# A two-layer hybrid decoder block on one core: both token tiles take turns on each tile of feed-forward weights, w2 in one-unit blocks, and a new order table

## The chip, the cores and the metric

The kernel runs on one core of a Trainium2 chip. The metric is the device time of one execution, in microseconds (us). Five engines matter: TensorE (PE, with its weight loads as PEld), VectorE (DVE), ScalarE (ACT), GpSimd (POOL) and SyncE (SP), which here issues the DMAs. The kernel before has a median of 1520.91 us.

## The reference

Two layers of a post-norm decoder, for 256 tokens of width 1024, all in float32 (a is a constant):

```
x = LN1(a*x + 0.5 * (silu(x @ w1) * (x @ w3)) @ w2)     FFN1, w1 and w3 1024 x 2816, w2 2816 x 1024
x = LN2(a*x + W_o(sum_i sigmoid(g_i(x)) * y_i(x)))      four gated token mixers: gMLP, short conv, MLA, NSA
x = LN3(a*x + CrossAttn(x, mem))                        4 heads over 256 memory rows
x = LN4(a*x + 0.5 * SwiGLU_2(x))                        FFN2, shapes of FFN1
```

## The kernel before

**Tiles.** The 256 tokens are two tiles of 128 (tile 0 and tile 1; `x_65` and `x_66` in the listings). A float32 product is made of three matmuls, from a high part and a low part of each operand: high by high (L256), high by low (L257), low by high (L258). For a feed-forward product the transposed tokens (`xh`, `xl`) are the operand that is loaded into TensorE and 512 columns of weights run past it.

**Weights.** They stream from memory once, in pieces of 128 x 1024 float32 (512 KB, two k-tiles of 512 columns each, or one k-tile of 1024 columns). A piece goes through three steps: a DMA issued by SP brings `raw` (4 buffers), ACT casts it to the high part `wh` (L244), DVE subtracts to get the low part `wl` (L245). `wh` and `wl` have 8 buffers each, the ring: a piece can be cast only when the piece that stood 8 before it has had its last matmul, and a `raw` buffer is free when its `wl` is made.

**A feed-forward.** Its 2816 hidden columns are five groups of 512 and one of 256 (`gi` 0 to 5 in `ffn`). In a group tile 0 first goes through all the pieces of w1 and w3 and then tile 1 does; only the first group of the whole kernel is written with both tiles at once. After a tile's two sums ACT makes `sil` (L407) and DVE `h` (L409), and `h` is transposed on TensorE a little later (it is deferred, and let out by `flush` within a later `group`). Then `wide` multiplies by w2: pieces ("units") of 2 k-tiles in blocks of 2, 3, 3 and 3 units, in each block tile 0 first, then tile 1, each with two 512-column sums. The layer norm (L361 to L369) adds the sums to x, and `to_xT` transposes x for the next stage.

**PSUM.** Three `acc` banks, one `oacc`, two `tr` (transposes) and two `att`.

**Order.** The program is not issued in the order of the code. `issue_order` takes a list per engine from the table `ISSUE`: numbers of the engine's instructions in program order, in the order in which they are to run. An engine runs its list strictly in order, so an instruction that waits holds up all that stand behind it on that engine. SP's list orders the DMA issues.

Other names below: `za`, `zb`, `zc`, `zd` are the first products of the mixing part, taken out of PSUM by DVE with a bias (L801, to `zza`, `zzb`, `zzc`, `zzd`); `gg`, `gb`, `bs`, `ws` are gMLP's parameters; `mq` is the rotated query (L466), `T` the gated sum of the mixers (L870), `xoh` the high part of the cross-attention output (L291), `xpT` its transposed probabilities (L972).

Of the kernel before, what the change touches and what calls it, by code (L numbers as in the profile page):

```python
# [17 lines left out]
P = 128  # L18
# [4 lines left out]
FF = 2816  # L23
# [4 lines left out]
NT = SEQ // P  # L28
KD = D // P
# [133 lines left out]
class Build:  # L163
# [38 lines left out]
    def acc(self):  # L202
        return self.ps.tile([P, 512], F32, name=self.nm("acc"), tag="acc", bufs=3)
# [172 lines left out]
    def ffn(self, l, which, lnw, last=False):  # L376
# [3 lines left out]
        for gi in range(6):  # L380
# [7 lines left out]
            first = len(self.plan) <= 4 and {t: (self.acc(), self.acc() if t == 0 else self.oacc()) for t in range(NT)}  # L388
            if first:
                for j, us in enumerate((u1, u3)):  # L390
                    for i, (get, k) in enumerate((get, k) for nk, get in us for k in range(nk)):
                        for t in range(NT):
                            self.mm3(first[t][j], *self.xT[t](i), *get(k, 0, w), i == 0, i == KD - 1)
            for t in range(NT):
                self.stream = "af"[t]
                if first:
                    pa, pb = first[t]
                elif w == 512:
                    pa, pb = self.acc(), self.acc() if t == 0 else self.oacc()
                    self.group(pa, self.xT[t], u1, 0, w)  # L400
                    self.group(pb, self.xT[t], u3, 0, w)
                elif w < 512:
                    both = self.acc()
                    self.group(both, self.xT[t], u13, 0, 2 * w)
                    pa, pb = both[:, :w], both[:, w:]
                sil = self.s("sil", w)
                nc.scalar.activation(sil, pa, AF.Silu)  # L407
                h = self.s("h", w)
                nc.vector.scalar_tensor_tensor(h, pb, 0.5, sil, op0=ALU.mult, op1=ALU.mult)  # L409
                hT[t, gi] = hh, hl = self.s("hh", w, F32R), self.s("hl", w, F32R)  # L410
                self.stream = "a"

                def back(h=h, hh=hh, hl=hl, w=w):
                    ps = self.transposes([h[:, i * P:(i + 1) * P] for i in range(w // P)])
                    self.split(ps[:, :w], hh, hl)
                self.later.append(back)
# [4 lines left out]
        out = self.wide(w2, l, FF // P, src, (2, 3, 3, 3))  # L421
# [604 lines left out]
def issue_order(tc, nc):  # L1026
# [3 lines left out]
    for engine in ENGINES:  # L1030
# [275 lines left out]
```

## Time and profile before

| what | value |
|---|---|
| median of 3 runs | 1520.91 us (1519.75 to 1523.56) |
| profiled execution, own time | 1518.77 us |
| its span, first to last instruction | 1517.0 us |
| mean granted TensorE clock | 0.998 |
| busy share PE, PEld, DVE, ACT | 98%, 82%, 66%, 47% |
| DMA queue of the weights, share of 16 engines | 55.2% |

The profile is one execution. Its own time is 2.1 us below the median, and 1.8 us above its span. A busy share counts the time from an instruction's start to its modelled end, and matmuls overlap, so the share says where TensorE is never idle and not how fast it goes; where it waits, a row of the trace carries the idle time and what ended it in square brackets.

### The profile page before, as it was taken

What the parts mean: (1) busy time and instruction counts of PE and PEld (TensorE: products, weight loads), DVE (VectorE), ACT (ScalarE), POOL (GpSimd) and SP (SyncE); (2) the same over time, 40 slices, a digit from 0 to 9 for tenths busy, and PEclk for the clock granted to TensorE, in tenths of its full rate; (3) what the DMA queues carried; (4) which work ended last, traced back from release to release, by engine and by line L of the source; (5) the groups of instructions that cost most, each with busy time, mean ns of one, the idle gap of its engine ahead of it and who ended that gap; (6) DMA issues with size and microseconds to landing.
All of it is one profiled execution on the core that took longest, in us unless ns stands there. A gap on an engine that the chain in (4) does not pass through costs nothing.

```text
span 1517.0 us, 20797 instructions
## 1 busy us (share of the span) xinstructions
PE 1488.4 (98%) x7994; PEld 1243.5 (82%) x7994; DVE 999.5 (66%) x1390; ACT 715.6 (47%) x1061; POOL 52.8 (3%) x48
## 2 busy tenths in 40 slices
PE   8999999999999999999999999999999999999998
PEld 6888788987887888878878887889778879888786
DVE  5555577888687776644665545787777777864535
ACT  5444433555456354543445443445555554554431
POOL 0000000000010000000000000000001100000000
PEclk9999999999999999999999999999999999999999
DMA  7566656445365554646556576654444565466533
GB/s 251 191 211 235 227 166 225 151 160 177 114 219 182 175 172 156 206 159 227 168 176 202 164 244 207 203 196 162 155 152 149 194 195 194 137 204 202 190 130 111
DMA packets 83187, 278.29 MB, mean 183 GB/s; under 512 B 10256, under 2 KB 11920, under 8 KB 83088
## 3 DMA queue, kind: packets, MB, share of 16 engines
q1 hardware_dynamic: 83088, 276.96, 55.2%
q8 instruction: 63, 1.03, 0.3%
q14 instruction: 36, 0.29, 0.1%
HBM read 275.88 MB, written 1.05 MB: 183 GB/s over the span
## 4 chain that ended last, share of the span: by engine, by line
PE 85%; DMA 7%; DVE 4%; ACT 2%; issue 1%; SPq 0%; POOL 0%; DVEq 0%; ACTq 0%
PE acc L256 21%; PE acc L258 21%; PE acc L257 21%; DMA raw<-in_wflat_dram 6%; PE oacc L257 4%; PE oacc L256 4%; PE oacc L258 4%; PE tr L306 4%; DVE wl L245 3%; ACT wh L244 2%; PE att L508 2%; PE oacc L521 1%; PE att L256 1%; PE att L258 1%; PE att L257 1%
## 5 line engine op out<-in xcount | busy, mean ns | idle before, releaser
L245 DVE TENSOR_TENSOR wl<-raw,wh 128x1024 fp32r<-128x1024 f32 (+4 forms) x487 | 585.6, 1220 | 289.8 <-ACT wh L244 280.9
L244 ACT CAST wh<-raw 128x1024 fp32r<-128x1024 f32 (+4 forms) x487 | 499.7, 1040 | 410.9 <-PE acc L258 247.8
L256 PE MATMUL acc<-wh,xh 128*128 128x512 f32 (+2 forms) x1008 | 389.8, 393 | 6.7 <-ACT wh L244 4.3
L257 PE MATMUL acc<-wl,xh 128*128 128x512 f32 (+2 forms) x1008 | 389.5, 390 | 0.6 <-DVE wl L245 0.6
L258 PE MATMUL acc<-wh,xl 128*128 128x512 f32 (+2 forms) x1008 | 388.3, 389 | 0.0
L256 PEld LDWEIGHTS acc<-wh,xh 128*128 128x128 f32 x1008 | 188.5, 188 | 48.5 <-ACT wh L244 8.5
L257 PEld LDWEIGHTS acc<-wl,xh 128*128 128x128 f32 x1008 | 189.8, 188 | 38.0 <-DVE wl L245 2.5
L258 PEld LDWEIGHTS acc<-wh,xl 128*128 128x128 f32 x1008 | 189.8, 188 | 36.4 <-issue 0.3
L257 PE MATMUL acc<-wl,hh 128*128 128x512 f32 x264 | 101.6, 392 | 1.7 <-DVE wl L245 1.7
L258 PE MATMUL acc<-wh,hl 128*128 128x512 f32 x264 | 101.9, 390 | 0.0
L256 PE MATMUL acc<-wh,hh 128*128 128x512 f32 x264 | 100.7, 396 | 0.0
L256 PE MATMUL acc<-xh,wh 128*128 128x256 f32 x320 | 90.8, 287 | 2.0 <-DVE zv L801 1.8
L257 PE MATMUL acc<-xl,wh 128*128 128x256 f32 x320 | 90.4, 285 | 0.0
L258 PE MATMUL acc<-xh,wl 128*128 128x256 f32 x320 | 90.0, 284 | 0.0
L256 PE MATMUL oacc<-wh,xh 128*128 128x512 f32 x176 | 69.7, 396 | 0.6 <-ACT wh L244 0.6
L257 PE MATMUL oacc<-wl,xh 128*128 128x512 f32 x176 | 69.4, 394 | 0.2 <-DVE wl L245 0.2
L258 PE MATMUL oacc<-wh,xl 128*128 128x512 f32 x176 | 69.3, 393 | 0.0
L256 PEld LDWEIGHTS acc<-xh,wh 128*128 128x128 f32 x320 | 61.0, 192 | 3.1 <-issue 2.5
L329 POOL TENSOR_TENSOR rstd<-var,cst 128x1 f32<-128x1 f32 x28 | 23.9, 860 | 1091.4 <-DVE var L328 1090.7
L257 PEld LDWEIGHTS acc<-xl,wh 128*128 128x128 f32 x320 | 61.2, 191 | 0.6 <-issue 0.3
L258 PEld LDWEIGHTS acc<-xh,wl 128*128 128x128 f32 x320 | 61.2, 192 | 0.1
L256 PEld LDWEIGHTS acc<-wh,hh 128*128 128x128 f32 x264 | 49.0, 188 | 13.9 <-ACT wh L244 4.9
(247 smaller groups left out, 1899.7 us busy)
## 6 DMA issues: line engine op xcount, KB each, us to landing
raw<-in_wflat_dram SPq DMA_DIRECT2D x465, 512.0 KB, 5.0
bias<-in_rows_dram SPq DMA_DIRECT2D x22, 256.0 KB, 5.6
lng<-in_rows_dram SPq DMA_DIRECT2D x8, 512.0 KB, 6.2
lnb<-in_rows_dram SPq DMA_DIRECT2D x8, 512.0 KB, 6.3
raw<-in_wflat_dram SPq DMA_DIRECT2D x8, 416.0 KB, 3.8
wc<-in_small_dram SPq DMA_DIRECT2D x8, 256.0 KB, 6.1
memr<-in_memt_dram SPq DMA_DIRECT2D x8, 256.0 KB, 6.0
raw<-in_wflat_dram SPq DMA_DIRECT2D x4, 420.0 KB, 3.4
```

Of the source, the lines that this page charges most:

```text
L244: nc.scalar.copy(hi[:, :m], raw[:, :m])
L245: nc.vector.tensor_sub(lo[:, :m], raw[:, :m], hi[:, :m])
L256: mm(out, ah, bh, start=start, stop=False, skip_group_check=True)
L257: mm(out, ah, bl, start=False, stop=False, skip_group_check=True)
L258: mm(out, al, bh, start=False, stop=stop, skip_group_check=True)
L306: self.nc.tensor.transpose(t[:rows, i * part:(i + 1) * part], s, self.ident[:part, :part])
L329: nc.gpsimd.tensor_tensor(y, v, self.c("mhalf"), op=ALU.pow)
L508: nc.tensor.matmul(ps[:, i * nk + s * P:i * nk + (s + 1) * P], qT(h0 + i), kT(h0 + i, s), start=True, stop=True, skip_group_check=True)
L521: nc.tensor.matmul(place(h), vT(h, s), p, start=s == 0 and start(h), stop=last and s == t, skip_group_check=True)
```

## The change

Three edits. First, in `ffn` the two tiles take turns on each k-tile of w1 and w3 (`turns`), in every group but the first one of the three later feed-forwards; the four sums are then open together, and deferred transposes are let out twice within a pass. Second, w2 runs in one-unit blocks, eight of them and a last one of three units: after each unit of 2 k-tiles the other tile follows on the same two pieces. Third, the table `ISSUE` is new for every engine, in all parts of the program. The arithmetic is the same: the same products, additions and DMAs.

```diff
-            first = len(self.plan) <= 4 and {t: (self.acc(), self.acc() if t == 0 else self.oacc()) for t in range(NT)}
-            if first:
-                for j, us in enumerate((u1, u3)):
-                    for i, (get, k) in enumerate((get, k) for nk, get in us for k in range(nk)):
-                        for t in range(NT):
-                            self.mm3(first[t][j], *self.xT[t](i), *get(k, 0, w), i == 0, i == KD - 1)
+
+            turns = gi > 0 or len(self.plan) <= 4
+            acc = lambda j, t: self.oacc() if j and t else self.acc()
+            ps = {}
+            if w == 512:
+                parts = [(j, us) for j, us in enumerate((u1, u3))]
+            else:
+                parts = [(0, u13)]
+            wide = 512
+            if turns:
+                for j, us in parts:
+                    for t in range(NT):
+                        ps[t, j] = acc(j, t)
+                    i = 0
+                    for nk, get in us:
+                        for k in range(nk):
+                            for t in range(NT):
+                                self.mm3(ps[t, j], *self.xT[t](i), *get(k, 0, wide), i == 0, i == KD - 1)
+                            i += 1
+                            if i in (DEFER, DEFER + 2):
+                                self.flush()
             for t in range(NT):
                 self.stream = "af"[t]
-                if first:
-                    pa, pb = first[t]
-                elif w == 512:
-                    pa, pb = self.acc(), self.acc() if t == 0 else self.oacc()
-                    self.group(pa, self.xT[t], u1, 0, w)
-                    self.group(pb, self.xT[t], u3, 0, w)
...
+                if not turns:
+                    for j, us in parts:
+                        ps[t, j] = acc(j, t)
+                        self.group(ps[t, j], self.xT[t], us, 0, wide)
...
-        out = self.wide(w2, l, FF // P, src, (2, 3, 3, 3))
+        out = self.wide(w2, l, FF // P, src, (1,) * 8 + (3,))
...
 ISSUE = {
     "PE":
-        "0-10 13 11-12 16 14 17-18 15 22 19-21 25 23-24 28-30 34-35 26-27 31-33 36 40-42 46 37 47-48 52-54 38-39 "
...
     "Pool":
-        "0-1 6-7 2-5 8-11 13 15 14 12 16-23 28-29 24-27 30-43",
+        "0-1 6-7 2-5 8-11 13-15 12 16-23 28-29 24-27 30-31 33-34 32 35-43",
```

Three places of the orders follow; the numbers behind a name tell copies apart. The first is TensorE in FFN1 of layer 0, second group of columns (`gi` = 1). `wh_280` and `wh_286` are pieces of w1, `wh_292` and `wh_304` pieces of w3; `acc_314` is tile 0's sum with w1. Before:

```order
L256 MATMUL acc_314<-wh_280,xh 128x512
L257 MATMUL acc_314<-wl_281,xh 128x512
L258 MATMUL acc_314<-wh_280,xl 128x512
L256 MATMUL acc_314<-wh_280,xh 128x512
L257 MATMUL acc_314<-wl_281,xh 128x512
L258 MATMUL acc_314<-wh_280,xl 128x512
L256 MATMUL acc_314<-wh_286,xh 128x512
```

After, where `acc_378` is tile 0's sum with w3 and `oacc_379` tile 1's:

```order
L256 MATMUL acc_378<-wh_304,xh 128x512
L256 MATMUL oacc_379<-wh_292,xh 128x512
L257 MATMUL acc_378<-wl_305,xh 128x512
L257 MATMUL oacc_379<-wl_293,xh 128x512
L258 MATMUL acc_378<-wh_304,xl 128x512
L258 MATMUL oacc_379<-wh_292,xl 128x512
L256 MATMUL acc_378<-wh_304,xh 128x512
L256 MATMUL oacc_379<-wh_292,xh 128x512
```

Before, one tile runs through a new piece every 6 matmuls; after, both tiles are on pieces that stand two apart, and a new piece is needed every 12.

The second place is DVE at the start of layer 0's mixing part: `wl_2086` to `wl_2098` are weights of `turned` products that run later, `zzc` are the additions that empty the PSUM banks of `zc`. Before:

```order
L245 TENSOR_TENSOR wl_2086<-raw_2083,wh_2085 128x1024
L245 TENSOR_TENSOR wl_2092<-raw_2089,wh_2091 128x1024
L801 TENSOR_TENSOR zzc_1772<-acc_1747,bias_1721 128x416
L801 TENSOR_TENSOR zzc_1799<-acc_1774,bias_1721 128x416
L245 TENSOR_TENSOR wl_2098<-raw_2095,wh_2097 128x1024
```

After:

```order
L245 TENSOR_TENSOR wl_2086<-raw_2083,wh_2085 128x1024
L814 TENSOR_TENSOR zzc_1772<-acc_1747,bias_1721 128x416
L814 TENSOR_TENSOR zzc_1799<-acc_1774,bias_1721 128x416
L245 TENSOR_TENSOR wl_2092<-raw_2089,wh_2091 128x1024
L245 TENSOR_TENSOR wl_2098<-raw_2095,wh_2097 128x1024
```

The two additions stand one weight piece earlier.

The third place is TensorE where FFN1 of layer 0 ends: `wh_1394` and `wh_1400` are the last pieces of w2, `x_65` is tile 0 after the layer norm, `acc_1586` the first sum of `za`. Before:

```order
L306 MATMUL tr_1491<-ident,x_65 128x128 x4
L257 MATMUL acc_1073<-wl_1395,hh_1065 128x512
L256 MATMUL acc_1074<-wh_1394,hh_1065 128x512
L258 MATMUL acc_1073<-wh_1394,hl_1066 128x512
L257 MATMUL acc_1074<-wl_1395,hh_1065 128x512
L256 MATMUL acc_1073<-wh_1400,hh_1065 128x512
L258 MATMUL acc_1074<-wh_1394,hl_1066 128x512
L257 MATMUL acc_1073<-wl_1401,hh_1065 128x512
L306 MATMUL tr_1498<-ident,x_65 128x128 x4
```

After:

```order
L256 MATMUL acc_1069<-wh_1394,hh_1060 128x512
L257 MATMUL acc_1069<-wl_1395,hh_1060 128x512
L258 MATMUL acc_1069<-wh_1394,hl_1061 128x512
L256 MATMUL acc_1069<-wh_1400,hh_1060 128x512
L257 MATMUL acc_1069<-wl_1401,hh_1060 128x512
L258 MATMUL acc_1069<-wh_1400,hl_1061 128x512
L306 MATMUL tr_1491<-ident,x_65 128x128 x4
L306 MATMUL tr_1498<-ident,x_65 128x128 x4
L256 MATMUL acc_1586<-wh_1538,xh 128x512
```

Tile 0's transposes moved from among the last w2 matmuls to behind them, and the product that reads them follows at once. Tile 1's transposes (`x_66`) stood 48 issues behind `wh_1538`'s first matmul and now stand 16 behind it.

Moves that are told in words: the DMAs of `gg`, `gb`, `bs` and `ws` stood between the last pieces of w2 on SP's list and now stand behind them, and in layer 1 DVE's `ws` operation (L721, now L734) stands behind the last `wl` of w2 instead of ahead of `wl_8049`; SP issues `raw_100` ahead of the tokens at the start; the cross-attention products of tile 1 and its transposes stand some 4 us of matmuls earlier; `mq`'s rotation is no longer split by other DVE work; in the last layer norm DVE's list had L368 twice and then L369 twice, and has L368, L369, L368, L369 after.

## Rows read from the trace of the kernel before

**Rows 1.** The page, busy time of each engine over the span.

```profile
PE 1488.4 (98%) x7994; PEld 1243.5 (82%) x7994; DVE 999.5 (66%) x1390; ACT 715.6 (47%) x1061; POOL 52.8 (3%) x48
```

**Rows 2.** TensorE's waits: us in total, times, longest us.

```profile
PE acc L256 <- ACT wh L244: 4.3, 5, 1.9
PE acc L257 <- DVE wl L245: 2.3, 3, 1.7
PE acc L256 <- DVE zzc L801: 2.1, 2, 1.5
PE tr L306 <- DVE mq L466: 1.4, 2, 0.9
PE acc L976 <- ACT xpT L972: 1.4, 2, 0.7
PE acc L256 <- ACT xoh L291: 1.4, 2, 0.7
PE oacc L256 <- ACT wh L244: 1.3, 3, 0.7
PE tr L306 <- DVE T L870: 0.8, 1, 0.8
PE oacc L257 <- DVE wl L245: 0.7, 2, 0.5
PE acc L258 <- DVE oCl L292: 0.5, 1, 0.5
PE acc L306 <- DVE h L409: 0.3, 1, 0.3
```

**Rows 3.** Timeline of PE in FFN1, steady: start us, us, instruction.

```profile
111.42 0.39 PE L256 MATMUL acc<-wh,xh 128*128 128x512 f32 x1
111.65 0.39 PE L257 MATMUL acc<-wl,xh 128*128 128x512 f32 x1
```

**Rows 4.** Timeline of PE at the supply waits of layer 0's FFN1.

```profile
23.24 0.39 PE L258 MATMUL acc<-wh,xl 128*128 128x512 f32 x1
24.48 0.73 PE L256 MATMUL acc<-wh,xh 128*128 128x512 f32 x2 [0.85 <-ACT wh L244]
...
30.78 0.73 PE L256 MATMUL acc<-wh,xh 128*128 128x512 f32 x2 [0.44 <-ACT wh L244]
32.04 0.50 PE L257 MATMUL acc<-wl,xh 128*128 128x512 f32 x1 [0.30 <-DVE wl L245]
```

**Rows 5.** Groups of DVE and ACT by form: count, busy us, mean ns, idle before.

```profile
L245 DVE TENSOR_TENSOR wl<-raw,wh 128x1024 fp32r<-128x1024 f32 x465 | 566.8, 1237 | 284.8 <-ACT wh L244 276.0 <-DMA raw<-in_wflat_dram 0.4
...
L244 ACT CAST wh<-raw 128x1024 fp32r<-128x1024 f32 x465 | 482.9, 1053 | 396.9 <-PE acc L258 237.4 <-DMA raw<-in_wflat_dram 68.7 <-PE oacc L258 35.1
...
L291 ACT CAST xh<-tr 128x512 fp32r<-128x512 f32 x28 | 15.8, 587 | 52.8 <-PE tr L306 52.6
```

**Rows 6.** The chain that ended last, at the end of layer 1's FFN1.

```profile
925.13 7.68 DMA ws<-in_small_dram
```

**Rows 7.** Timeline of DVE at layer 0's `zzc`.

```profile
233.93 1.23 DVE L245 TENSOR_TENSOR wl<-raw,wh 128x1024 fp32r<-128x1024 f32 x1 [1.96 <-ACT wh L244]
235.07 1.08 DVE L801 TENSOR_TENSOR zzc<-acc,bias 128x416 f32<-128x416 f32 x2
```

**Rows 8.** Timeline of ACT in layer 1's FFN2, w2.

```profile
1427.90 1.06 ACT L244 CAST wh<-raw 128x1024 fp32r<-128x1024 f32 x1 [0.30 <-PE acc L258]
1429.26 1.05 ACT L244 CAST wh<-raw 128x1024 fp32r<-128x1024 f32 x1 [0.30 <-PE acc L258]
```

**Rows 9.** Timeline at the end, behind the last matmul.

```profile
1509.49 0.69 DVE L361 SCALAR_TENSOR_TENSOR x<-x,acc 128x512 f32<-128x512 f32 x1 [2.22 <-PE acc L258]
...
1511.25 1.40 DVE L368 SCALAR_TENSOR_TENSOR x<-x,mv,lng 128x512 f32<-128x512 f32 x2
1511.48 0.92 POOL L329 TENSOR_TENSOR rstd<-var,cst 128x1 f32<-128x1 f32 x1 [7.78 <-DVE var L328]
1512.57 1.41 DVE L369 SCALAR_TENSOR_TENSOR x<-x,rstd,lnb 128x512 f32<-128x512 f32 x2
```

More of the change, by code (lines that the diff above doesn't have):

```diff
@@ L387, in ffn @@
                 u13 = self.cols((w1, w3), l, c0, 2 * w, KD)
-            first = len(self.plan) <= 4 and {t: (self.acc(), self.acc() if t == 0 else self.oacc()) for t in range(NT)}
-            if first:
-                for j, us in enumerate((u1, u3)):
-                    for i, (get, k) in enumerate((get, k) for nk, get in us for k in range(nk)):
-                        for t in range(NT):
-                            self.mm3(first[t][j], *self.xT[t](i), *get(k, 0, w), i == 0, i == KD - 1)
+            turns = gi > 0 or len(self.plan) <= 4
[18 more added lines that the diff above has]
+                                self.flush()
             for t in range(NT):
                 self.stream = "af"[t]
-                if first:
-                    pa, pb = first[t]
-                elif w == 512:
-                    pa, pb = self.acc(), self.acc() if t == 0 else self.oacc()
-                    self.group(pa, self.xT[t], u1, 0, w)
-                    self.group(pb, self.xT[t], u3, 0, w)
[L402 to L405, printed above, removed]
+                if not turns:
+                    for j, us in parts:
+                        ps[t, j] = acc(j, t)
+                        self.group(ps[t, j], self.xT[t], us, 0, wide)
+                if w == 512:
+                    pa, pb = ps[t, 0], ps[t, 1]
+                else:
+                    pa, pb = ps[t, 0][:, :w], ps[t, 0][:, w:]
                 sil = self.s("sil", w)
```

388 rows, old and new, of the table ISSUE are left out of this document.

## The prediction

> **What bounds the kernel now.** I read the page first: TensorE is busy 98% of the span, the others far less [rows 1]. Neither that share nor a faster engine elsewhere says what can be won; what can is TensorE's idle time, so the view that counts is its list of waits [rows 2]. The rows there that the change can reach add up to 16.5 us in 26 waits. The timeline of a steady stretch gives the pace: a 512-column matmul starts every 0.23 us [rows 3], and a piece of weights lasts 12 of them, 2.7 us, when both tiles use it together, but 1.36 us when one tile runs through it alone. The groups show what a piece costs to make: 1.05 us on ACT, 1.24 us on DVE, and that most of ACT's idle time ahead of its casts ends with a matmul, that is, with a slot of the ring coming free, not with a DMA [rows 5]. So the ring is the supply's limit in most places, and the order decides how often a piece is wanted right behind the one whose slot it takes.
>
> A wait costs more than its idle time: at the first one of FFN1 the starts are 1.24 us apart, 1.01 more than the pace, with 0.85 us idle [rows 4]. I add 0.16 us per wait throughout.
>
> **The change part by part.** The instructions are the same in number and shape on every engine that matters, so no busy time is added or removed; the sum is made of waits.
>
> *Feed-forwards in turns (FFN1).* Layer 0 has three waits at 24 to 32 us, 0.85, 0.44 and 0.30 us [rows 4], all in the second group, where tile 0 alone runs through eight new pieces at 1.36 us each. In the new order that group starts some 30 issues later, and counting 0.227 us per matmul, no slot in either FFN1 is wanted less than 4 us after its old piece's last use; before, 20 pieces of layer 0 and 23 of layer 1 were wanted within 2.6 us. A cast and a subtraction together take 2.3 us, so those waits go: 1.59 + 3 x 0.16 = 2.1 us. In layer 1 the longest wait for `wl` (1.7 us) has another root: the chain leads to the DMA of `ws`, which took 7.7 us [rows 6], because DVE's operation on it stood ahead of a weight's subtraction. It now stands behind the last one: 1.9 us. The wait for `h` (0.3), the shorter of `oacc`'s two for `wl` (0.7 less 0.5) and the shortest of its three for `wh` (I take 0.2 of the 0.6 that the longest leaves) also lie in FFN1 [rows 2]: 0.7 + 3 x 0.16 = 1.2 us. Together **-5.1**. Of the five waits of `acc` for `wh` (4.3 us) the start (1.9) is another matter, and two of 1.1 us together lie in the first group of layer 1, still tile after tile: nothing for them.
>
> *w2 in one-unit blocks (FFN2).* In FFN2 the new order doesn't relax the ring. Counting as above, 36 pieces of the two FFN2 are wanted 1.36 us after their slot's last use, before 29. A cast (1.05 us) fits with 0.3 us to spare: before, two casts follow each other in just this rhythm, ACT 0.30 us idle and released by a matmul each time [rows 8]. The longer waits of `oacc` for `wh` and `wl` (0.7 and 0.5 us) lie here. I leave them as they are: **0**; the bounds are -2 (they go) and a rival below.
>
> *Mixing and cross-attention, by the table alone.* `zzc`: in layer 0 a subtraction, itself 1.96 us late behind a cast, stood ahead of the two additions that empty PSUM for `zd` [rows 7]; the additions now stand ahead of it, and were ready. 2.1 + 2 x 0.16 = **-2.4**. `xoh`: the products it waits for run 4 us earlier, against 0.7 us of wait: **-1.7** (1.4 and two times 0.16). `T` and `oCl`, whose cover by count grows to 3.9 and 7.5 us: 1.3 + 0.32 = **-1.6**. `mq`: its rotation now runs together on DVE, which shortens the chain but doesn't move TensorE's transposes much: half of 1.7, **-0.9**, between 0 and -1.7. `xpT`: its transposes move up but a copy of the values now ends 0.1 us ahead of its use by count, so the wait gets another name: **-0.2**, between 0 and -1.7 [rows 2]. Start: the first weight is issued and cast first; I take one cast of tokens, 0.59 us [rows 5], off the 1.9 us: **-0.6**.
>
> *What it adds.* The seam from FFN1 to `za` in each layer. Before, tile 0's transposes ran among the last w2 matmuls, and tile 1's were 48 issues (11 us) behind the first product. Now nothing stands between tile 0's second transposes and the matmul that reads their copy. A cast of this size takes 0.59 us [rows 5]; some of it lies beside the eight transposes themselves, so 0.4 us, and 0.1 to 0.3 more when the low part is wanted. Tile 1's chain is longer: from the start of its first addition to `rstd` 1.99 us, `rstd` 0.92 and the last scaling 0.7 us, with hand-offs 3.8 us to the first half of x [rows 9], plus two subtractions of tile 0's split that DVE's list puts among them, about 0.7 each as L361 is: near 5.1 us, against 4.5 us of matmuls from the last w2 sum to its transposes. That is 0.5 us, in all 1.0 per layer: **+2.0** (0 to +4). The same pattern with tile 0 only stands between layer 0's FFN2 and layer 1's FFN1: **+0.4**. Tail: DVE ran L368 twice while POOL made `rstd`, then L369 twice [rows 9]; with L368, L369, L368, L369 the second L368 (0.7 us) slides behind `rstd`: **+0.7**. Four accumulations open at once and orders this tight will have some wait that counting misses: **+1.2**, a bare reserve between 0 and +8.
>
> A sum can only start when the bank that it takes has been read out. By the listing FFN1's banks come round 5 to 11 us after their last sum ends, the readers are short (0.69 us for an operation like L361 [rows 9]), and the one wait behind such a reader is 0.3 us now (`h`) [rows 2]; so I put nothing on it, and the far end is a rival. The Trainium skill, "Perfetto Trace Analysis", section "Optimizing Tensor Performance", asks that independent groups of matmuls rotate through different PSUM banks, so that emptying one overlaps the next group; four sums that open and close nearly together rotate less than two and two. By that rule the turns would cost at each group's end, and the sum would be that of rival 3; no run here shows it yet.
>
> **The sum.** Removed 5.1 + 2.4 + 1.7 + 1.6 + 0.9 + 0.2 + 0.6 = 12.5; added 2.0 + 0.4 + 0.7 + 1.2 = 4.3; net -8.2 us. The profiled execution took 1518.8 us, so it would take 1510.6; the median of the runs is 2.1 us above it, which gives **1512.7 us**. A difference of 0.3%, 4.6 us, is about what a measurement of this kernel can tell from none.
>
> **The rivals.**
> 1. *Given back at the seams, no measurable change.* The seams between stages take 4 us per layer and not 1 (both tiles' chains are late, and DVE's weights queue behind the waiting norm steps), or the reserve is 6. Then 12.5 - 9 leaves -3: about 1518 us. For it speaks how near the cover is to the chain (4.5 against 5.1 us); against it, that DVE is idle a third of the span [rows 1] and that a reserve of 6 has no row behind it.
> 2. *The ring in w2 binds: slower.* The 36 pieces wanted 1.36 us behind their slots have 0.3 us to spare. If hand-offs use it up, each comes late, and each delay is paid on TensorE. It decides at 8.2 / 36 = 0.23 us each, where the gain is gone; at 0.4 us each, 14.4 - 8.2 gives +6, 1527 us. Against it: 29 such pieces cost two or three waits before.
> 3. *Banks not free in turns: slower.* Four sums end nearly together, and the next group's first sum waits for a reader of its bank, once in each of the 17 groups of 512 columns in turns. At one reader and a wait's cost, 0.69 + 0.16, it is +14.5 less 8.2: about +6, 1527 us; it decides at 0.48 us each. Against it: the 5 to 11 us above.
> 4. *Nearly all waits go.* The order hides the seams, FFN2's waits go as well, `mq` and `xpT` too: 16.5 + 26 x 0.16 = 20.7 us off, less 2 or 3 of new ones: about 1503 us.
>
> **How the numbers follow.** My forecast (1508 to 1516 us) has 0.50, no measurable change 0.19, the ring in w2 0.06, the banks 0.04, nearly all gone 0.21. The first and the last are faster: 0.71, less a little for the forecast's upper edge, 0.69; same 0.21; slower 0.10. The range leaves the slow rivals and the far end of rival 4 out: 1503 to 1521 us; the forecast alone spans 1508 to 1516.
>
> **What would show it.** TensorE's waits for `wh` and `wl` in FFN1 beyond the start and layer 1's first group absent; no `zzc`, `xoh`, `T` or `oCl` in the list; `xh` and an `x` of the layer norm new in it, near 186 us and in layer 1's seam, under 1.2 us per seam; `oacc` for `wh` and `wl` in FFN2 near 2 us; the time behind the last matmul 0.7 us longer; the busy columns' counts unchanged. It is wrong if waits for weights are as many as before under other names, if waits for `h` or `sil` multiply, or if DVE is late at the seams by more than 2 us each.

## The result and the profile after

The kernel after takes 1503.22 us, median of 4 runs (1501.73 to 1504.53); the kernel before, run beside it, 1520.42 us (1519.75 to 1523.56). The ratio is 0.9883, 95% interval [0.9865, 0.9900]: 17.2 us less, where 8.2 were forecast for the profiled execution. The time lies at the lower edge of the range, and its size is that of rival 4 (about 1503 us).

The profiled execution of after took 1504.53 us over a span of 1502.8 us, 14.2 us less than the one of before. It is the slowest of after's four runs, while before's profiled one lies 1.7 us below the median; so 3 of the 17.2 us are spread between runs, and the traces can explain 14.2.

The page of after, busy time of each engine, beside [rows 1]:

```profile
PE 1482.7 (99%) x7994; PEld 1246.7 (83%) x7994; DVE 999.3 (66%) x1390; ACT 720.1 (48%) x1061; POOL 52.6 (3%) x48
```

The counts are unchanged, and the share of TensorE goes from 98% to 99%, which doesn't say where the 1% was won. Its list of waits says more (us in total, times, longest), beside [rows 2]:

```profile
PE acc L989 <- ACT xpT L985: 2.3, 2, 1.2
PE acc L256 <- ACT xh L291: 2.2, 4, 1.5
PE acc L256 <- DVE zv L814: 2.0, 2, 1.1
PE acc L750 <- DVE zv L741: 1.8, 4, 0.9
PE acc L1010 <- DVE zpT L778: 1.1, 1, 1.1
PE att L256 <- ACT memh L291: 0.7, 1, 0.7
PE acc L257 <- DVE wl L245: 0.5, 1, 0.5
PE tr L306 <- DVE mq L479: 0.5, 1, 0.5
PE tr L306 <- DVE mk L711: 0.2, 1, 0.2
PE acc L258 <- DVE wl L245: 0.2, 1, 0.2
```

Waits for `wh` are gone, and of those for `wl` 0.7 us are left, 0.5 at the start and 0.2 in the mixing part. (Of the 2.2 us for `xh`, 1.5 are the start of the kernel and 0.2 stand at each of three seams.) The whole list falls from 21.0 to 11.5 us. That is 9.5 us less idle time for 14.2 us less span, so a third of the gain has no idle time in the rows of the matmuls. Windows over the feed-forwards show it. Columns: stretch, its length, busy time and (count) of PE, then PEld, DVE, ACT and POOL, granted clock, DMA share, GB/s. First before, in FFN1 of layer 0 and of layer 1:

```profile
18.00:193.00 175.00, 173.26 (x774) 139.25 (x773) 95.13 (x95) 78.55 (x88) 0.00 (x0) 1.00 0.65 219
760.00:930.00 170.00, 168.38 (x759) 135.82 (x758) 90.83 (x94) 72.84 (x85) 0.92 (x1) 1.00 0.60 198
```

The same windows of after:

```profile
18.00:193.00 175.00, 175.00 (x795) 144.90 (x794) 99.57 (x100) 81.42 (x91) 0.99 (x1) 1.00 0.65 220
760.00:930.00 170.00, 170.00 (x775) 140.54 (x774) 92.96 (x93) 76.20 (x85) 0.49 (x1) 1.00 0.64 208
```

In the first window before idles 1.74 us, but issues 21 matmuls fewer, which at the pace of 0.227 us [rows 3] are 4.8 us; in the second 1.62 us and 16 matmuls, 3.6 us. (Some of them are short transposes, so these are rough.) What the missing 3 and 2 us look like is seen just behind the first wait of [rows 4], in before's timeline of PE and of PEld, the loads that stand ahead of the matmuls:

```profile
24.48 0.73 PE L256 MATMUL acc<-wh,xh 128*128 128x512 f32 x2 [0.85 <-ACT wh L244]
...
25.73 0.19 PEld L257 LDWEIGHTS acc<-wl,xh 128*128 128x128 f32 x1 [0.27 <-DVE wl L245]
25.74 0.49 PE L257 MATMUL acc<-wl,xh 128*128 128x512 f32 x1
26.07 0.39 PE L258 MATMUL acc<-wh,xl 128*128 128x512 f32 x1
```

From 25.74 to 26.07 a matmul takes 0.33 us instead of 0.23, with no bracket on a matmul: the stall is shorter than the overlap of two matmuls, and the matmul's row only reads 0.49 instead of 0.39. The bracket stands on the load, which here waits for `wl` though it loads `xh`. So the list of the loads counts what the list of the matmuls leaves out. Between 18 and 193 us before has

```profile
PEld acc L256 <- ACT wh L244: 5.1, 17, 1.3
PEld acc L257 <- DVE wl L245: 1.0, 2, 0.7
PEld oacc L257 <- DVE wl L245: 0.9, 2, 0.6
```

and after has no load there that waits for `wh` or `wl`. Of these 21 waits four also leave a matmul idle. The cost of one is read from the start times: the starts of the matmul that waits and of the two behind it, less the pace. The four cost 2.9 us and the seventeen 1.1. Over all four feed-forwards before has 53 such waits: 11 that leave a matmul idle cost 9.5 us, the other 42 cost 3.0. After has 17, none of which leaves a matmul idle; they cost 1.1 us. That is 11.4 of the 13.3 us that the table below gives the feed-forwards. (Starts over 0.30 us apart without idle time are no measure of it: between 18 and 185 us before has 22 and after 10, but 15 of the 22 and all 10 come right behind short transposes.)

Laid side by side by the same matmuls (the time of each in its trace, stage by stage), the traces differ thus, in us, rounded; the last column is an experiment told below:

| stage | predicted | after | ring9 |
|---|---|---|---|
| start | -0.6 | -0.8 | -0.5 |
| FFN1, layer 0 | -2.1 | -4.6 | -2.4 |
| FFN1, layer 1 | -1.9 | -5.9 | -5.2 |
| FFN1, not placed | -1.2 | | |
| FFN2, both layers | 0 | -1.1 and -1.7 | -0.8 and -1.9 |
| seams FFN1 to `za`, two | +2.0 | +1.7 | 0.0 |
| seam FFN2 to FFN1 | +0.4 | +0.6 | 0.0 |
| mixing and cross-attention, both layers | -6.8 | -2.9 and -0.2 | -2.6 and -1.6 |
| behind the last matmul | +0.7 | +0.65 | |
| reserve | +1.2 | | |
| sum | -8.2 | -14.2 | -15.1 |

### The profile page after: what moved, and what is told of

The parts are those of the page before. It is cut to its first block, busy times and chain, and to the rows that moved or that the text cites. A ratio compares the mean times of both kernels' runs of the same rounds, so it can differ in the third digit from the quotient of the medians.

```text
span 1502.8 us, 20807 instructions
## 1 busy us (share of the span) xinstructions
PE 1482.7 (99%) x7994; PEld 1246.7 (83%) x7994; DVE 999.3 (66%) x1390; ACT 720.1 (48%) x1061; POOL 52.6 (3%) x48
## 4 chain that ended last, share of the span: by engine, by line
PE 92%; DMA 4%; DVE 2%; ACT 1%; issue 1%; POOL 0%; SPq 0%; POOLq 0%; ACTq 0%; DVEq 0%
PE acc L256 23%; PE acc L258 23%; PE acc L257 23%; PE oacc L256 4%; PE oacc L257 4%; PE tr L306 4%; PE oacc L258 4%; DMA raw<-in_wflat_dram 3%; PE att L521 2%; PE oacc L534 1%; ACT wh L244 1%; DVE wl L245 1%; PE att L256 1%; PE att L258 1%; PE att L257 1%
## 5 line engine op out<-in xcount | busy, mean ns | idle before, releaser
L257 PEld LDWEIGHTS acc<-wl,hh 128*128 128x128 f32 x264 | 49.6, 188 | 10.5
```

The lines of the kernel that those rows point to most:

```text
L257: mm(out, ah, bl, start=False, stop=False, skip_group_check=True)
```

## The experiments

Each ratio is to the kernel before, run beside it.

| run | median, us | ratio [95%] |
|---|---|---|
| before_free | 1629.35 | 1.0724 [1.0702, 1.0746] |
| after_free | 1617.10 | 1.0647 [1.0630, 1.0664] |
| turns_free | 1616.86 | 1.0641 [1.0622, 1.0661] |
| blocks_free | 1625.58 | 1.0714 [1.0685, 1.0743] |
| ring9 | 1505.41 | 0.9899 [0.9883, 0.9915] |
| small_bufs | 1518.80 | 0.9993 [0.9978, 1.0007] |
| repairs | 1521.86 | 1.0007 [0.9996, 1.0019] |
| plus | 1502.10 | 0.9875 [0.9854, 0.9895] |
| turn4 | 1507.35 | 0.9921 [0.9908, 0.9933] |
| after_w2_blocks | 1503.61 | 0.9900 [0.9883, 0.9916] |
| after_ring9 | 1498.51 | 0.9858 [0.9843, 0.9873] |

**The edits without the table.** Four kernels drop the table and run in the order that the scheduler gives:

```diff
-            issue_order(tc, nc)
```

before_free and after_free are the two kernels so; turns_free has the turns alone, with w2 in blocks `(2, 3, 3, 3)`; blocks_free has w2's `(1,) * 8 + (3,)` alone.

> The kernel before without its order table: the instructions go in the order that the scheduler gives them by itself. It is the base for the three runs beside it. Both theories: slower than the kernel before, by 15 to 80 us, with more waits for wh and wl.

> The changed kernel without its order table. Theory code (the turns themselves relieve the supply, whatever the table, because a piece is done with after one go of both tiles and more of the ring is free to run ahead): 8 us or more below the kernel before without its table, with the difference in the feed-forwards. Rival table (the gain is that of the new order, and the code only allows it): within 4 us of it.

> The turns alone, w2 in blocks of 2, 3, 3 and 3 units as before, no order table. Theory code: nearly all of the difference between the two kernels without table, 6 us or more below the kernel before without its table. Rival: w2 in small blocks is what helps, then it is within 3 us of it.

> w2 in one-unit blocks alone, tile after tile in w1 and w3, no order table. Theory code: within 3 us of the kernel before without its table, since in my count the w2 blocks relieve nothing. Rival: 5 us or more below it.

before_free is 111 us slower than before, where 15 to 80 were expected, and its matmuls wait less for `wh` and `wl`, not more: 4.5 us against 8.6. The turns alone are worth 12.5 us (1629.35 to 1616.86), the blocks of w2 nothing beyond the spread, alone (3.8 us, intervals that overlap) or on top of the turns (+0.2 us). But this gain is not the one looked for. In this order TensorE's waits are other ones; the first and the fifth of before_free:

```profile
PE acc L256 <- ACT xh L291: 14.9, 2, 10.9
...
PE tr L306 <- DVE h L409: 5.3, 14, 0.8
```

The 14 waits for `h` are absent with turns; with before's table that wait is 0.3 us [rows 2]. The waits for `wh` and `wl` hardly change with turns (4.5 and 4.2 us). So the runs show that turns pay without a table, and in the main not through the supply; where the rest of the 12.5 us lies is not shown. What they pay under the table has to be tested under it.

**One more pair in the ring, the order untouched.** The theory from here on: a piece can be cast only when a pair of `wh` and `wl` is free, and before holds its pairs so long that many pieces are ready only just in time; the turns and the new table give the pairs back sooner. If so, a ninth pair must do the same to the kernel before. ring9 pays for it with scratch buffers; small_bufs has the smaller scratch buffers alone.

```diff
-RING_BUFS = 8
-SA_BUFS = 24
-SF_BUFS = 17
+RING_BUFS = 9
+SA_BUFS = 22
+SF_BUFS = 16
-... tag="tiny" + self.stream, bufs=24 if self.stream == "a" else 16)
+... tag="tiny" + self.stream, bufs=20 if self.stream == "a" else 16)
```

> The kernel before, its order table untouched, with nine pairs of weight buffers instead of eight (room made by fewer scratch buffers). Theory look-ahead (in the order before, a piece of FFN1 lives 16 us in the ring from its first to its last use, so hardly a slot is left to run ahead, and that is what costs the waits): a slot more gives each piece about 2.7 us more, and the waits for wh and wl in the feed-forwards mostly go: 4 to 8 us faster. Rival order (the table holds the casts back, or the transfers do, whatever the ring): within 2 us of the kernel before.

> The control for the run with nine: the same fewer scratch buffers, with the eight pairs of before. Both theories: within 2 us of the kernel before.

ring9 gains 15 us, more than the 4 to 8 that were expected, with not one instruction moved, and small_bufs nothing. Its windows:

```profile
18.00:193.00 175.00, 174.09 (x785) 142.55 (x784) 97.31 (x99) 80.61 (x92) 0.99 (x1) 1.00 0.66 220
760.00:930.00 170.00, 169.81 (x773) 139.64 (x772) 91.24 (x93) 75.41 (x87) 0.74 (x1) 1.00 0.62 205
```

785 and 773 matmuls, against 774 and 759 before and 795 and 775 after: in layer 1's FFN1 the ninth pair does nearly all that the change does. The column ring9 of the table above has its gains in the same stages as after's. What it does not have is after's seams (+2.3 us), since its order is before's. Its waits at `zzc` fell from 2.1 us in two to

```profile
PE acc L256 <- DVE zzc L801: 0.5, 1, 0.5
```

so that wait was a late weight too, and not the order on DVE.

**Two repairs of the table alone.** The kernel before, with two of the moves that the prediction priced, both on DVE alone: the additions to `zzc` one subtraction earlier in both layers, and the operation on `ws` behind the last weights of layer 1's w2. (The DMAs of `ws` and its neighbours already stood behind those weights in SP's list, which is unchanged.) On DVE:

```diff
-L245 TENSOR_TENSOR wl_2092<-raw_2089,wh_2091 128x1024
 L801 TENSOR_TENSOR zzc_1772<-acc_1747,bias_1721 128x416
 L801 TENSOR_TENSOR zzc_1799<-acc_1774,bias_1721 128x416
+L245 TENSOR_TENSOR wl_2092<-raw_2089,wh_2091 128x1024
...
-L721 TENSOR_TENSOR ws_8371<-ws_8371,cst 128x512
 L245 TENSOR_TENSOR wl_8049<-raw_8046,wh_8048 128x1024
 L245 TENSOR_TENSOR wl_8055<-raw_8052,wh_8054 128x1024
 L245 TENSOR_TENSOR wl_8061<-raw_8058,wh_8060 128x1024
+L721 TENSOR_TENSOR ws_8371<-ws_8371,cst 128x512
```

> The kernel before with two repairs of its order and nothing else: the additions zzc one weight piece earlier on VectorE in both layers, and in layer 1 the DMAs of gg, gb, bs and ws and the operation on ws behind the last piece of w2. Theory, by the terms of the prediction: -2.4 and -1.9, about 4.3 us faster, and the two waits absent. Rival: the time is taken by the next wait in line, under 1.5 us faster.

No gain. The wait behind `ws` went, 1.9 us as priced (the longest wait for `wl` on the list falls from 1.7 to 0.4 us), but the next stage gave it back, and the `zzc` waits stayed:

```profile
PE acc L256 <- DVE zzc L801: 3.4, 2, 2.2
PE tr L306 <- DVE zza L466: 2.8, 2, 2.3
```

Where the new wait for `zza` comes from is seen in layer 1, on DVE's timeline and then on SP's:

```profile
986.39 1.09 DVE L801 TENSOR_TENSOR zzc<-acc,bias 128x416 f32<-128x416 f32 x2 [2.82 <-DMA bias<-in_rows_dram]
987.40 4.09 DVE L245 TENSOR_TENSOR wl<-raw,wh 128x1024 fp32r<-128x1024 f32 x4
994.29 0.81 DVE L801 TENSOR_TENSOR zzd<-acc,bias 128x280 f32<-128x280 f32 x2 [2.81 <-DMA bias<-in_rows_dram]
```

```profile
982.46 6.51 SPq L241 DMA_DIRECT2D raw<-in_wflat_dram  x3
989.06 0.59 SPq L218 DMA_DIRECT2D bias<-in_rows_dram  x1
```

The additions, now first, wait 2.82 us for their bias and hold up the subtractions behind them. These give the `raw` buffers back later, so SP's three issues of `raw` take 6.51 us (3.68 before), the next bias is issued 2 us later (989.06; before 987.04), `zzd` waits for it, and `zza` behind it is 2.3 us late for TensorE.

**More of the same on the kernel after.** plus moves tile 0's transposes at the seam forward in w2, with their copies, and puts the tail's operations back into before's order:

```diff
+L306 MATMUL tr_1491<-ident,x_65 128x128 x4
 L256 MATMUL acc_1069<-wh_1382,hh_960 128x512
...
+L306 MATMUL tr_1498<-ident,x_65 128x128 x4
...
-L306 MATMUL tr_1491<-ident,x_65 128x128 x4
-L306 MATMUL tr_1498<-ident,x_65 128x128 x4
 L256 MATMUL acc_1586<-wh_1538,xh 128x512
```

> The changed kernel with its two seams and its tail mended: at the end of FFN1 in both layers tile 0's transposes, casts and subtractions stand among the last matmuls of w2 again, and the last layer norm runs L368, L368, L369, L369. Theory: two times 0.88 us of the seams and 0.65 us of the tail, 2 to 2.5 us faster than the changed kernel, some 1501 us. Rival: the DVE work moved ahead delays tile 1's chain by as much, then only the tail, 0.7 us.

1.1 us below after, where 2 to 2.5 were expected; the intervals don't tell it from nothing. The wait for `xh` at the seam went, and 4 to 7 us later TensorE waited ahead of tile 1's transposes instead (0.71 us in layer 0, 0.54 in layer 1, there for DVE's `x`): tile 1's chain of the layer norm is the next to be late.

**Is it the turn on each tile, or only the pairs coming free?** turn4 keeps after's table elsewhere, but lets tile 0 go through four pieces before tile 1 takes the same four, in all feed-forwards. TensorE's order at the first group in turns:

```diff
 L256 MATMUL acc_314<-wh_268,xh 128x512
+L257 MATMUL acc_314<-wl_269,xh 128x512
...
+L256 MATMUL acc_314<-wh_274,xh 128x512
...
 L256 MATMUL acc_315<-wh_268,xh 128x512
```

> The kernel after with a longer stay of each piece in the ring: in every feed-forward tile 0 goes through four pieces of weights before tile 1 takes the same four, so that a piece is used for about 10 us instead of 5 to 6 us; w2 stays in one-unit blocks, the work outside the feed-forwards keeps its order. Theory that the gain comes from the pieces that stand ready in the ring: five pieces or fewer are then ready ahead instead of about seven, still more than before had at most places, so most of the gain stays: 0.988 to 0.991 of before (up to 4 us slower than the kernel after). Rival, that taking turns itself is what pays (each weight tile used twice in a row, whatever stands ready): the feed-forwards of before come back, 0.995 to 0.998 of before.

0.9921, just above the first theory's 0.991, which the interval holds, and below the rival's 0.995. Its windows over the two FFN1:

```profile
18.00:193.00 175.00, 175.00 (x795) 145.00 (x794) 97.70 (x101) 79.08 (x90) 0.99 (x1) 1.00 0.66 220
760.00:930.00 170.00, 170.00 (x775) 140.59 (x774) 91.89 (x93) 74.43 (x85) 0.78 (x1) 1.00 0.65 209
```

These are after's counts to the matmul. A piece of w1 and w3 stays in use longer there, on the mean 6.5 us instead of 4.1 in layer 0 and 8.3 instead of 6.3 in layer 1 (from its first matmul to its last; before has 14.6 and 15.9), and it costs nothing. The stay is shorter than the 10 us that were expected, so the test is milder than planned. What turn4 loses, it loses elsewhere; the rows of its list of waits that after doesn't have, with 3.9 us:

```profile
PE tr L306 <- DVE h L422: 2.5, 2, 1.7
PE oacc L256 <- DVE h L422: 1.0, 1, 1.0
PE oacc L257 <- DVE wl L245: 0.4, 1, 0.4
```

Three of the four are waits for `h`, the longest of them in the second FFN2, on DVE's timeline:

```profile
1361.29 1.23 DVE L245 TENSOR_TENSOR wl<-raw,wh 128x1024 fp32r<-128x1024 f32 x1 [0.71 <-ACT wh L244]
1362.43 0.68 DVE L422 SCALAR_TENSOR_TENSOR h<-oacc,sil 128x512 f32<-128x512 f32 x1
```

and on PE's:

```profile
1363.77 1.09 PE L306 MATMUL tr<-ident,h 128*128 128x128 f32 x8 [1.69 <-DVE h L422]
```

`h` stands behind a subtraction for a later weight in DVE's list, and TensorE's transposes of it stand where the turns of after had covered it. So in FFN1 not the shortest possible stay of a piece is needed, but that it be short enough; and the order of `h` against the transposes is part of the price.

**w2's blocks under the new table.** The kernel after, with w2 in blocks of 2, 3, 3 and 3 units in TensorE's list alone; written as blocks of the code, it is

```diff
-(1,) * 8 + (3,)
+(2, 3, 3, 3)
```

> The kernel after with w2 back in blocks of 2, 3, 3 and 3 units (only the order of w2's own matmuls on TensorE is changed, in all four feed-forwards; everything else is issued where the kernel after has it). Theory that what pays is how long before its use a piece stands ready: a w2 piece stays in the ring several us longer, so the casts behind it come later, and the waits of before's second feed-forwards come back in part: 3 to 6 us slower than the kernel after, 0.990 to 0.993 of before. Rival, as the prediction's term for w2 had it (0): the blocks of w2 don't matter beside the turns in w1 and w3, 0.987 to 0.9895 of before.

The time is the rival's: 1503.61 us beside after's 1503.22. The ratio, 0.9900, is the lower edge of the theory's range, but the medians are 0.4 us apart.

The edit does what its text says in FFN1 alone. There after issues w2 in one-unit blocks, and with this edit a piece of w2 stays 10.2 us instead of 6.7; the windows over FFN1 keep after's 795 and 775 matmuls. So one-unit blocks are not where FFN1's gain comes from.

In FFN2 it does the reverse, for the kernel after doesn't issue one-unit blocks there. The code has them, but the table has the last word: it lets tile 0's first sum run seven pieces of w2 ahead of the other three sums, as before's table did by eight. A piece of w2 stays 20.7 us in layer 0's FFN2 and 19.7 in layer 1's (before 18.5 and 20.4); with this edit it stays 11.3 and 10.5 us. Pieces that in after were ready 1.3 and 1.9 us ahead of use are ready 10.1 us ahead, and the waits of `oacc`'s loads that after has in FFN2, in layer 0 and in layer 1,

```profile
PEld oacc L256 <- ACT wh L244: 1.5, 7, 0.2
PEld oacc L256 <- ACT wh L244: 1.6, 8, 0.2
```

are gone. The windows from 577 to 740 and from 1330 to 1480 us, full in both kernels, hold 3 matmuls more each (738 for 735, 684 for 681). What that wins is lost at the seam behind layer 0's FFN2, where TensorE's transposes of x now wait 1.6 us for DVE. So FFN2's gain can't come from one-unit blocks either: after doesn't run them there.

**Nine pairs under the new table.** The buffers of ring9 in the kernel after.

> The kernel after with nine pairs of wh and wl instead of eight (and the smaller scratch buffers that pay for them). Theory that the changed kernel has no supply wait left in its feed-forwards: a ninth pair buys at most the two waits at the start of the second feed-forward of before's kind, 0 to 2 us, ratio to before 0.987 to 0.989. Rival, that the ninth pair and the turns remove different stalls and so add up: 0.978 to 0.982 of before, about 15 us below the kernel after.

1498.51 us, the fastest of all: 4.7 us below after by the medians (3.8 by the ratios), more than the first theory's 2 and far from the rival's 15. The two remedies don't add up in FFN1:

```profile
18.00:193.00 175.00, 175.00 (x795) 144.99 (x794) 97.76 (x100) 80.44 (x91) 0.99 (x1) 1.00 0.66 219
760.00:930.00 170.00, 170.00 (x774) 140.59 (x773) 92.64 (x95) 75.00 (x86) 0.92 (x1) 1.00 0.61 203
```

The same counts as after's, to one matmul. A part comes from FFN2, where after's waiting loads are gone and the windows named above hold 4 and 3 matmuls more (739 and 684). The larger part comes from the mixing parts, whose weights go through the same ring: from 210 to 500 us after issues 1828 matmuls and after_ring9

```profile
210.00:500.00 290.00, 288.75 (x1840) 248.18 (x1839) 221.28 (x378) 152.71 (x282) 18.99 (x14) 1.00 0.54 178
```

Not all of that is the ninth pair's. turn4 and after_w2_blocks, which have eight pairs and after's order there, issue 1831 and 1833; in layer 1, from 950 to 1240 us, both issue 1834, after 1828 and after_ring9 1835.

## Why the prediction came out as it did

**The bound was read rightly.** "The ring is the supply's limit in most places": ring9 shows it, since one more pair alone is worth 15 us. In after the supply runs ahead. The groups of [rows 5] now read

```profile
L245 DVE TENSOR_TENSOR wl<-raw,wh 128x1024 fp32r<-128x1024 f32 x465 | 566.1, 1226 | 335.7 <-ACT wh L244 324.1 <-PE acc L258 1.7 <-PE acc L257 1.2
L244 ACT CAST wh<-raw 128x1024 fp32r<-128x1024 f32 x465 | 485.0, 1052 | 460.9 <-PE acc L258 271.0 <-PE oacc L258 91.4 <-DMA raw<-in_wflat_dram 45.2
```

The casts are idle 64 us more, 90 us more of it for TensorE to free a pair (362.4 us against 272.5) and 24 less for a DMA: ACT waits for TensorE, and TensorE's matmuls no longer for ACT's casts. Matching each cast with the first matmul that reads it, the first three pieces left out, a piece of layer 0's FFN1 was ready 3.9 us ahead on the mean before and 14.6 after; 26 of 63 pieces were less than 1 us ahead before, and none after. In ring9 it is 5.1 us, with 11 of 63 under 1 us.

**The step that failed: the sum over the feed-forwards, "Together -5.1" in FFN1 and "0" in FFN2.** They gave 13.3 us. The mechanism was the one named; the size was short by 8.2 us, in three ways. First, "the sum is made of waits", and the list that it was taken from holds the matmuls' idle time alone. The first wait of [rows 4] idles 0.85 us and costs 1.01 at its own matmul and 0.1 at the next, and the eleven waits of this kind cost on the mean 0.28 us more than their idle time, not "0.16 us per wait". Beside them seventeen loads of layer 0's FFN1 and ten of layer 1's wait without leaving a matmul idle, which costs 1.1 and 0.7 us. Layer 0's FFN1 gave 4.6 us, not 2.1. Second, layer 1's first group, "still tile after tile: nothing for them", gave 1.8 us, though the change doesn't take turns in it; ring9, whose group is the same, gained 1.7 there. What came before it decides how far ahead its pieces are. Third, FFN2's 36 pieces wanted 1.36 us behind their slots were taken as a reason for no gain. The count was right, since w2's order in FFN2 is hardly changed: in after 18 and 16 pieces there are less than 1 us ahead. But they come only a little late. The two FFN2 had 18 loads that waited for `wh` or `wl` before, the longest 1.2 us, and they cost 3.7 us; after has 17, none over 0.2 us, which cost 1.1. FFN2 gave 2.8 us. Which share of it the turns in w1 and w3 have and which the rest of the table, no run here tells apart.

The list of waits was a lower bound on what the supply cost. The Trainium skill, "Perfetto Trace Analysis", section "Optimization Strategy", says that the same gap repeating on the engine that should be saturated can mean too few buffers for the next tile. The cause holds here, as ring9 shows, and the sign is in the trace, though not where the prediction looked: among the matmuls before's gaps were few and of all sizes (thirteen waits for `wh` and `wl` [rows 2]), but among the loads twelve wait 0.18 to 0.21 us each for `wh` between 149 and 186 us.

**Mixing and cross-attention: -6.8 predicted, -3.1 found.** `T`, `xoh` and `oCl` went as said, and `mq` to 0.5 us, the half that was taken. `zzc`'s -2.4 was a wrong root: the additions moved ahead of a late subtraction, but what they wait behind was late because of the ring. repairs moved them and kept the wait; ring9 moved nothing and lost most of it. In after the 2.1 us of that stage in layer 0 are won, and 1.4 of them are lost in the next, where `zv` stands behind another late subtraction. DVE's timeline:

```profile
239.49 1.23 DVE L245 TENSOR_TENSOR wl<-raw,wh 128x1024 fp32r<-128x1024 f32 x1 [2.03 <-ACT wh L244]
240.63 0.69 DVE L814 TENSOR_TENSOR zv<-acc,bias 128x512 f32<-128x512 f32 x1
...
243.55 0.75 DVE L741 SCALAR_TENSOR_TENSOR zv<-zv,rstd,gb 128x512 f32<-128x512 f32 x1 [0.44 <-POOL rstd L329]
```

and PE's:

```profile
244.36 0.71 PE L750 MATMUL acc<-ws,zv 128*128 128x128 f32 x4 [0.93 <-DVE zv L741]
```

That is [rows 7] again, a little later and with another name. The order alone doesn't decide it: turn4 and after_w2_blocks have the same order there and 0.5 us of waits for this `zv` (L741) where after has 1.8. `xpT` got worse, 2.3 us instead of 1.4, where -0.2 was forecast.

**Right in size.** The start (-0.8 for -0.6) is so by luck in part, since the clock has a hand in it (last section). The seams (+1.7 for +2.0; +0.6 for +0.4) are, and the tail, where the second L368 slid behind `rstd` as told:

```profile
1497.54 0.75 DVE L369 SCALAR_TENSOR_TENSOR x<-x,rstd,lnb 128x512 f32<-128x512 f32 x1 [0.44 <-POOL rstd L329]
1498.21 0.74 DVE L368 SCALAR_TENSOR_TENSOR x<-x,mv,lng 128x512 f32<-128x512 f32 x1
```

From the start of the last matmul to the end of the execution it is 0.65 us longer (1504.53 less 1494.17, against 1518.77 less 1509.06). The errors add up: 8.2 too little in the feed-forwards, 3.7 too much in the rest, 1.2 of reserve not needed, 0.3 in the small ones, together 6.0 of the 14.2.

**The rivals.** Rival 4 came true in size, though not as it was worked out: its sum held every listed wait (24 by [rows 2], not 26), of which `xpT`, `mq` and the seams remained, and nothing for the loads that wait without an idle matmul. Rival 2, the ring in w2, left its trace in the loads alone: fifteen of w2 wait 0.2 us each in after's FFN2, at a cost of some 0.06 us, where the rival needed 0.23 to cancel the gain. Rival 3, the banks, left none: after's list has no wait for `sil` or `h`. By the rule of the Trainium skill that stood behind rival 3 ("Perfetto Trace Analysis", "Optimizing Tensor Performance", independent groups rotate through different PSUM banks) the turns would have cost at each group's end; with 5 to 11 us between the end of a sum and the next use of its bank, no row shows that they do.

## What to carry to other kernels

Where tiles go through a ring of buffers, look at how far ahead of its use a tile is ready, and not only at the matmuls' waits in the list: read the waits of the weight loads as well, and count the matmuls of equal windows. Where a table sets the order, read the order as it is issued: here the code's one-unit blocks of w2 run in FFN1 alone. The quickest test of such a theory is one more buffer with the order untouched and, beside it, the buffers that pay for it taken away alone; here that test gave nearly as much as a change of three edits, and both together gave a little more. A wait that a local reorder removes is worth its price only if its root was in that place: where the root is a common supply, the wait moves to the next name, and an operation that is put ahead of the supply's own work holds up the buffers and the DMA queue behind it.

## What the runs showed of the hardware

A short stall of TensorE leaves no idle time in the rows of its matmuls: with 0.39 us for a matmul and a start each 0.23 us, a start that is 0.1 us late shows in the start times, and as a bracket on the load that waited (0.27 us at 25.73 above). Nothing in the busy share (98 and 99%) told of it.

The clock at the start comes and goes between executions. In before's profile the granted clock was 0.51 (about 1.2 of 2.4 GHz) from 8.0 to 11.4 us, behind 1.89 us in which TensorE was idle:

```profile
8.00:11.40 3.40, 3.40 (x8) 2.38 (x9) 1.09 (x2) 1.42 (x2) 0.00 (x0) 0.51 1.01 374
```

Its matmuls start 0.43 us apart there instead of 0.23. ring9 and repairs, with before's order at the start, read 1.00 in this window, but the starts say otherwise: they too are 0.43 us apart until 10.1 and 10.3 us, as in repairs' timeline of PE:

```profile
8.60 0.63 PE L257 MATMUL acc<-wl,xh 128*128 128x512 f32 x1
9.03 0.63 PE L258 MATMUL acc<-wh,xl 128*128 128x512 f32 x1
```

after reads 1.00 and starts a matmul each 0.23 us from 8.25 us on. after_ring9, the fastest kernel of all, has its order and reads 0.56. The 41st 512-column matmul on an `acc` bank starts at 17.48 us in after, at 17.84 and 18.17 in plus and after_ring9, whose starts are slow, and at 18.26 in before. So some 0.4 to 0.7 of the 14.2 us between the two traces are the clock's and no part of the change's gain.
